# Group 1's operands written where they are multiplied, one transfer for a row's two operands, group 0's second operands in later windows

## The chip, the cores and the metric

The kernel runs on one core of a Trainium2 chip. That core has five engines which each work through a list of instructions of their own in order: PE (products and transposes), DVE and ACT (element-wise work), POOL (here mostly casts) and SP (which issues nearly all transfers). The metric is the device time of one execution in microseconds. The order of every list is fixed when the program is built; what an instruction waits for is a semaphore of another engine or of a transfer.

## The reference

One layer of a hybrid backbone over 2048 latent tokens and 256 context tokens, width 1024:

```python
h  = rmsnorm(x, norm_w)  * (1 + scale) + shift        # 2048 x 1024
hc = rmsnorm(ctx, norm_w) * (1 + scale_c) + shift_c   # 256 x 1024
p, pc = h @ w_in, hc @ w_in[:, :HG_COLS]              # w_in: 1024 x 9216
# 8 heads of 128: S_t = diag(f_t) S_{t-1} + k_t v_t^T, o_t = S_t^T q_t,
# forward and backward, each from the state that the context leaves
y_hg = hgrn_out(o, gate)
y_cv = conv_branch(p[..., HG_COLS:])
y = concatenate([y_hg, y_cv]) @ w_out
return rmsnorm(x + gate_ada * y, final_norm_w)
```

scale, shift and gate come from a small product of the conditioning vector with w_ada ("ada").

## The kernel before

**Tiling.** The 2048 tokens are four groups of 512 (x0 to x3), the context a fifth block of 256. A window is one column block (a head, later a convolution channel block) with one group: head 0 meets groups 0, 1, 2, 3 in windows 0 to 3, and the next blocks run through the groups in turn. A window consists of units, each the product of one pair of 128-column weight blocks with the group. Weights and tokens are held as two float16 halves, hi and lo, and each product is three matmuls: hi by hi, hi by lo, lo by hi (L890 to L892).

**Products.** Most units ("head", "conv") use a scheme of seven products in place of eight on blocks of 2 by 2 (`seven`). A group's side of it are the seven operands B11, T1, T2, B21, T3, B22 and T4, each 512 by 256: the four quarters of h, transposed, and their sums and differences. The names in the trace drop the digits: hop1B is any of window 1's B11, B21 and B22, hop1T any of its T1 to T4. In window 0 the four units are "plain" (eight products, L1419 to L1421), on operands that stay in four tiles hop0. Three "ctx" units (L1405 to L1407) are multiplied with the context's operands, tile hc.

**Making operands.** `norm_group` loads the tokens (L234), squares them on ACT with a sum per row (L238), takes the reciprocal root in a chain of small rows on DVE (L125 to L131), scales the rows on ACT (L244) and DVE (L246), turns them on PE (xT_x, L253), scales by column on ACT (L274), and `combine` makes sums and differences on DVE (L328 to L337). `store2` casts hi on ACT or POOL (L279, L281), subtracts for lo on DVE (L298) and stores the operand to DRAM, tile Hd (L300). One turn is one k of four, that is 128 rows of each half. `prefetch` loads an operand from Hd into one of nine tiles named hop (L1306) when a tile comes free and the group is ready. The second operands of group 0 (T1 to T4), not needed by plain units, are made from a copy of h in DRAM (Xd) by `late_turn`; their tiles on DVE are ha_x, hb_x and ht_x.

**Order.** `run` walks a window's units. Steps of other work, each with a weight (PACE), are placed between its products in proportion to their weight: a chain (the scan of the window before, and head 0's context) and extra steps. Before:

- window 0: four plain and three ctx units; as extra steps the context's norm and turns, x1's norm and turns, x2's loads, norm and first turn;
- window 1: the other turns of x2, then x3's loads, norm and first turn;
- window 2: the other turns of x3;
- window 3: group 0's `late_turn`, four times, and the sums of the final gate (w_ada's last third, gate_r).

A weight pair is loaded, its power-of-two scale taken (ss_p on PE from rb_p on DVE) and split into hi and lo while an earlier unit runs. Head 0's outputs are o_0, o_1 and so on, one for each group, on PE.

The windows' extra steps are chosen here:

```python
early = (ctx_norm[1] + ctx_norm[2] + n1[1] + n1[2] if wi == 0 else n1[2][1:]) + ready_
...
elif wi == NG - 1:
    extra = first[3] + extra
```

Of the kernel before, what the change touches and what calls it, by code (L numbers as in the profile page):

```python
# [9 lines left out]
F32 = mybir.dt.float32  # L10
# [9 lines left out]
P = 128  # L20
# [40 lines left out]
def hybrid_layer(ctx: ExitStack, tc, x, cx, w_ada, b_ada, w_in, w_out, fnorm_w, small_d, masks, ident_d, sel_d, out):  # L61
# [19 lines left out]
    Hd = [{o: dp.tile([P, 2, HK, HW], F16, name=f"Hd{g}{o}", tag=f"Hd{g}{o}") for o in OPS} for g in range(NG)]  # L81
# [32 lines left out]

    def hop_tile(nm):
        return hp.tile([P, 2, HK, HW], F16, tag="hop", name=nm)
# [90 lines left out]
    def modulate_end(pada):  # L207
        ada_r = ring("ada_r")
        V.tensor_copy(ada_r, pada)
        ptr = pa_t("ada_t")  # L210
        for q in range(4):
            PE.transpose(ptr[:, q * P:(q + 1) * P], ada_r[:, q * P:(q + 1) * P], ident)
        V.tensor_tensor(ada, ptr.rearrange("p (q j m) -> p j q m", q=4, j=4)[:, :, :, 0:2],
                        sub(bada, 0, [[4, 4], [1, 4], [0, 2]]), ALU.add)

# [10 lines left out]
    def norm_group(ntile, src, row0, m, nm, first_ops=None, space=q_tile):  # L226
        n = ntile * P
        xs = []
        ssq = sp.tile([P, 16], F32, tag="ssq", name=f"ssq_{nm}", bufs=4)

# [6 lines left out]
        def square(i):  # L237
            S.activation(junk, xs[i], AF.Square, accum_out=ssq[:, i:i + 1])  # L238

        def norm():  # L240
            rstd = rsqrt(ssq[:, :ntile], ntile, 1.0 / D, nm)
# [8 lines left out]
        def transposed(k):  # L250
            pt = pa_t(f"xT_{nm}{k}")
# [4 lines left out]
        def raw(k):  # L256
            pt = transposed(k)
            raws[k] = ring(f"h32_{nm}{k}")
            if k % 2:
# [17 lines left out]
        def cast(eng, hi, src):  # L277
            if eng is G:
                G.tensor_scalar(hi, src, 1.0, 0.0, ALU.mult, ALU.add)  # L279
            else:  # L280
                S.activation(hi, src, AF.Copy)  # L281

        def store(op, k, src, eng):
# [3 lines left out]
            else:  # L287
                hi, lo = [first_ops[k // 2][:, i, k % 2] for i in range(2)]
            cast(eng, hi, src)
            V.tensor_tensor(lo, src, hi, ALU.subtract)  # L290

        def store2(ops, k, row, eng):

            n2 = len(ops)
            pair = hp.tile([P, 2, n2, HW], F16, tag="pair", name=f"hp{ops[0]}_{nm}{k}", bufs=4)
            hi, lo = [pair[:, i].rearrange("p a b -> p (a b)") for i in range(2)]
            cast(eng, hi, row)
            V.tensor_tensor(lo, row, hi, ALU.subtract)  # L298
            for i, op in enumerate(ops):
                SY.dma_start(Hd[row0 // GW][op][:, :, k], pair[:, :, i])  # L300
# [23 lines left out]
        def combine(k, a, b, whole):  # L324
# [10 lines left out]
            else:  # L335
# [8 lines left out]
                [paced(0.0, lambda k=k: raw(k)) for k in range(KT)])  # L344
# [12 lines left out]
    def behind(fn):  # L357

        if not last_keep:
            return fn()  # L360
        with tc.issue_after(last_keep[-1].ins):
            fn()
# [583 lines left out]
    def load_C(pool, tp, names):  # L946

        for o in names:
            C[tp][o] = pool.tile([P, 2, HK, GW], F16, name=f"C{tp}{o}")
# [74 lines left out]
    def wo_at(name, hl, k):  # L1024
        return wo_home(name, hl)[:, k // HK, k % HK, :]
# [160 lines left out]
    for wi, (kind, a, i) in enumerate(stretch):  # L1186
        units, chain, extra = [], [], []
        if kind == "head":
# [4 lines left out]
            if wi == 0:  # L1193
                units += [(zk, "plain", 1, lambda ps, w, s_=sg_: s_.gate_in(0, ps, w)),
                          (zk, "plain", 2, lambda ps, w, s_=sg_: s_.gate_in(1, ps, w)),
                          (vk, "plain", 1, sg_.value_in), (vk, "plain", 2, sg_.query_in),
                          (zk, "ctx", 1, lambda ps, w, c_=c_: c_.gate_in(0, ps, w)),
                          (zk, "ctx", 2, lambda ps, w, c_=c_: c_.gate_in(1, ps, w)), (vk, "ctx", 1, c_.value_in)]
            else:
                units.append((zk, "head", g, sg_.gates))  # L1200
                if i == 0:
                    units += [(zk, "ctx", 1, lambda ps, w, c_=c_: c_.gate_in(0, ps, w)),
                              (zk, "ctx", 2, lambda ps, w, c_=c_: c_.gate_in(1, ps, w))]
                units.append((vk, "head", g, sg_.values))
# [4 lines left out]
            if i == 1:  # L1209
# [8 lines left out]
        if wi > 0 and stretch[wi - 1][0] == "head":  # L1218
            _, pa_h, pi = stretch[wi - 1]
            chain += scan_steps(heads[pa_h], heads[pa_h].segs[pi])  # L1220
# [77 lines left out]
    for wi, g in enumerate(group_of):  # L1298
        if g is not None and wi and g != group_of[wi - 1]:
# [10 lines left out]
    x1_norm = norm_group(NCH, x, GW, 0, "x1", None, wa_hop)  # L1310
    plain = [hp.tile([P, 2, 2, GW], F16, tag="hop", name=f"hop0_{i}") for i in range(KT // 2)]
    a21_ = hop_tile("a21")
    extra_a21 = [[a21_[:, hl, :, i * P:(i + 1) * P] for hl in range(2)] for i in range(2)]
    taken[0] = len(plain) + 1 + NCH
# [11 lines left out]
    pada = modulate(lambda k: first[4][k][1](), lambda: next_w(0))  # L1326
# [272 lines left out]
```

## Time and profile before

| | us |
|---|---|
| median of three runs (lowest, highest) | 2181.78 (2180.26, 2185.07) |
| the profiled run: time, span | 2187.49, 2185.7 |
| PE, PEld busy in the span | 2089.4, 1468.2 |
| DVE, ACT, POOL busy | 1652.1, 1169.2, 157.9 |
| transfers: all 16 engines, mean | 142 GB/s |

The profile is of one execution, which took 2187.49 us. Busy time of an engine leaves out the time in which it waits. A wait is put down to what released it last ("PE xT_x L253 <- DVE xt_x L246": PE's row of line 253 waited for DVE's row of line 246). A row in the timelines has the start, the duration, the engine, the line, what is written and read, and in brackets the idle time just ahead of it. Matmuls overlap: what is shown as 0.27 long starts 0.11 after the one before.

### The profile page before, as it was taken

What the parts mean: (1) busy time and instruction counts of PE and PEld (TensorE: products, weight loads), DVE (VectorE), ACT (ScalarE), POOL (GpSimd) and SP (SyncE); (2) the same over time, 40 slices, a digit from 0 to 9 for tenths busy, and PEclk for the clock granted to TensorE, in tenths of its full rate; (3) what the DMA queues carried; (4) which work ended last, traced back from release to release, by engine and by line L of the source; (5) the groups of instructions that cost most, each with busy time, mean ns of one, the idle gap of its engine ahead of it and who ended that gap; (6) DMA issues with size and microseconds to landing.
All of it is one profiled execution on the core that took longest, in us unless ns stands there. A gap on an engine that the chain in (4) does not pass through costs nothing.

```text
span 2185.7 us, 51899 instructions
## 1 busy us (share of the span) xinstructions
PE 2089.4 (96%) x21563; PEld 1468.2 (67%) x21563; DVE 1652.1 (76%) x3456; ACT 1169.2 (53%) x2341; POOL 157.9 (7%) x239
## 2 busy tenths in 40 slices
PE   5789999999999999999999999999999999999998
PEld 2677688888887988888889887444444444444443
DVE  7887777878779778788687786677787656687775
ACT  7865556666557565666675654344444423333332
POOL 0211111010010110101111000000000000000000
PEclk9999999999999999999999999999999999999999
DMA  9766533433243333333633448923443205633321
GB/s 349 238 205 208 181 132 103 141 116 105 86 159 107 114 114 125 111 108 128 194 123 123 140 156 260 274 97 121 135 139 98 66 30 181 213 124 108 127 85 58
DMA packets 196464, 310.41 MB, mean 142 GB/s; under 512 B 13570, under 2 KB 126594, under 8 KB 194436
## 3 DMA queue, kind: packets, MB, share of 16 engines
q1 hardware_dynamic: 194068, 303.16, 42.5%
q8 instruction: 169, 2.77, 0.5%
q10 hardware_dynamic: 2160, 3.93, 0.5%
q14 instruction: 67, 0.55, 0.1%
HBM read 241.77 MB, written 65.27 MB: 140 GB/s over the span
## 4 chain that ended last, share of the span: by engine, by line
PE 66%; DVE 18%; ACT 8%; DMA 5%; issue 2%; POOL 1%; SPq 0%; POOLq 0%; ACTq 0%; DVEq 0%
PE sa L890 8%; PE sa L891 8%; PE sa L892 8%; PE sb L890 4%; PE sb L891 4%; PE sb L892 4%; PE sa_o L890 2%; PE sa_o L891 2%; PE sa_o L892 2%; DVE e_p L152 2%; PE A L599 2%; PE sc L890 2%; PE sc L892 2%; PE sc L891 2%; DVE K L453 2%
## 5 line engine op out<-in xcount | busy, mean ns | idle before, releaser
L453 DVE TENSOR_TENSOR K<-K,tot 128x512 f32<-128x512 f32 x192 | 133.6, 696 | 60.1 <-PE A L627 27.6
L891 PEld LDWEIGHTS <-e_p 128*128 128x128 f16 x1368 | 134.1, 98 | 60.4 <-issue 10.9
L890 PEld LDWEIGHTS <-e_p 128*128 128x128 f16 x1368 | 134.1, 98 | 59.9 <-DMA hop1T<-Hd1T 2.6
L892 PEld LDWEIGHTS <-e_p 128*128 128x128 f16 x1368 | 134.2, 98 | 52.8 <-issue 1.8
L460 DVE TENSOR_TENSOR Q<-Q,tot 128x512 f32<-128x512 f32 x192 | 132.4, 690 | 44.3 <-PE A L599 30.9
L569 ACT ACTIVATE km<-K 128x512 f32<-128x512 f32 x160 | 109.0, 686 | 69.5 <-DVE K L453 60.0
L890 PEld LDWEIGHTS <-whib_p 128*128 128x128 f16 x912 | 89.3, 98 | 41.2 <-issue 5.0
L890 PEld LDWEIGHTS <-whia_p 128*128 128x128 f16 x912 | 89.4, 98 | 38.5 <-DMA hop3B<-Hd3B 2.8
L891 PEld LDWEIGHTS <-whib_p 128*128 128x128 f16 x912 | 89.4, 98 | 38.2 <-issue 4.1
L891 PEld LDWEIGHTS <-whia_p 128*128 128x128 f16 x912 | 89.3, 98 | 37.7 <-issue 5.6
L892 PEld LDWEIGHTS <-wlob_p 128*128 128x128 f16 x912 | 89.4, 98 | 34.7 <-issue 0.5
L892 PEld LDWEIGHTS <-wloa_p 128*128 128x128 f16 x912 | 89.4, 98 | 34.4
L151 ACT ACTIVATE e_p<-ws_p,sc_p 128x512 f16<-128x512 f32 x108 | 77.2, 717 | 53.4 <-DVE ws_p L413 33.3
L576 POOL COPY qm<-Q 128x512 f32<-128x512 f32 x64 | 55.7, 870 | 630.2 <-DVE Q L460 627.2
L635 POOL COPY A<-Ac 32x128 f32<-32x128 f32 x128 | 68.3, 534 | 371.2 <-ACT A L631 367.2
L897 ACT ACTIVATE u<-sa,sx_w 128x256 f32<-128x256 f32 (+1 forms) x114 | 59.8, 525 | 59.2 <-PE sa L892 48.7
L897 ACT ACTIVATE p<-sb,sx_w 128x256 f32<-128x256 f32 (+1 forms) x114 | 59.4, 521 | 52.9 <-PE sb L892 52.3
L897 ACT ACTIVATE p<-sa,sx_w 128x256 f32<-128x256 f32 (+1 forms) x114 | 59.1, 518 | 47.4 <-PE sa L892 46.6
L152 DVE SCALAR_TENSOR_TENSOR e_p<-ws_p,sc_p,e_p 128x512 f16<-128x512 f32 x108 | 78.5, 742 | 1.0 <-ACT e_p L151 1.0
L813 ACT ACTIVATE cv<-c,small 128x512 f32<-128x512 f32 (+1 forms) x36 | 24.2, 674 | 97.6 <-DVE c L831 52.9
L378 ACT ACTIVATE junk<-ws_p 128x1024 f16<-128x1024 f32 x72 | 75.7, 1051 | 0.2
L151 ACT ACTIVATE hiS_o<-y_o,sc_y 128x1024 f16<-128x1024 f32 x32 | 36.8, 1149 | 72.6 <-PE sa_o L891 32.2
(865 smaller groups left out, 6972.1 us busy)
## 6 DMA issues: line engine op xcount, KB each, us to landing
ws_p<-in_w_in SPq DMA_DIRECT2D x72, 512.0 KB, 4.4
y_o<-yT SPq DMA_DIRECT2D x32, 512.0 KB, 4.2
xt_x<-in_x SPq DMA_DIRECT2D x16, 512.0 KB, 4.6
wa<-in_w_ada SPq DMA_DIRECT2D x16, 512.0 KB, 10.2
Gd<-zs SPq DMA_DIRECT2D x32, 256.0 KB, 3.2
wos<-in_w_out SPq DMA_DIRECT2D x32, 256.0 KB, 3.9
sg<-Gd SPq DMA_DIRECT2D x32, 256.0 KB, 3.8
yT<-y SPq DMA_DIRECT2D x32, 256.0 KB, 2.2
```

What stands on the lines that cost most here:

```text
L151: S.activation(hi, src, AF.Copy, scale=st[:, 0:1])
L152: V.scalar_tensor_tensor(lo, src, st[:, 0:1], hi, ALU.mult, ALU.subtract)
L378: S.activation(junk.rearrange("p (k n) -> p k n", k=KT), stage[i], AF.Abs, accum_out=r)
L453: V.tensor_tensor(m, m, sub(cur, nb + 1, [[2, np_], [-(nb + 1), 2], [0, B]]), ALU.mult)
L460: V.tensor_tensor(m, m, sub(cur, 1, [[2, np_], [nb - 1, 2], [0, B]]), ALU.mult)
L569: S.activation(sub(s.km, 0, [[2 * B, n // (2 * B)], [B, 2], [1, B]]), mix(s.K, n, B, n // (2 * B)), AF.Copy)
L576: G.tensor_copy(sub(qm, 0, [[2 * B, n // (2 * B)], [B, 2], [1, B]]), mix(s.qf, n, B, n // (2 * B)))
L635: G.tensor_copy(A3[js, :, js], s.Ac[js])
L890: PE.matmul(ps, hi[:, k], rh, start=start and k == 0, stop=False, skip_group_check=not start)
L891: PE.matmul(ps, hi[:, k], right(name, 1, k), start=False, stop=False, skip_group_check=not start)
L892: PE.matmul(ps, lo[:, k], rh, start=False, stop=k == nk - 1, skip_group_check=not start)
L897: last_keep.append(S.activation(r, ps, AF.Copy, scale=sx))
```

## The change

1. Group 1's seven operands are written straight into the tiles from which they are multiplied in window 1, own1: four of the hop tiles and three tiles of the kind Q. `store2` has a branch for that (direct): a cast and a difference for each operand of 128x256, and no store. When window 1 begins, `store_own` writes all seven to DRAM, for the later windows. The rows of x1 are loaded into tiles of their own ("stage"), ahead of the context's; x2's go to the tiles that x1 had.
2. The context's squares, norm, turns and its three units move from window 0 to window 1: two units behind the first unit on group 1, the third ahead of the second one. `context_steps` stand in window 1's chain, ahead of the last two scan steps.
3. x2's loads, norm and all four turns stand in window 1, x3's loads and norm at its end or behind, and x3's turns, all four, in window 2.
4. Operands that are made from one row, (B11, T3), (T1, T2) and (B21, B22), share a DRAM tile, Hr, with the halves hi and lo next to each other: one transfer of 128x1024 for a pair instead of two of 256x1x256. A load of an operand that shares a tile is 128x8x256 instead of 128x2048.
5. `late_turn` moves from window 3 to windows 4 and 5, two of the four k in each.
6. At the start: ada_r is copied in halves by DVE and ACT; group 0's last two transposes stand behind ada's, and ACT copies them; the context's half of `affine` stands behind the third of group 0's differences; a group's squares stand behind the casts of the group before and its norm behind that group's differences (`follow`).

The diff, cut:

```diff
+    ROWS = (("B11", "T3"), ("T1", "T2"), ("B21", "B22"), ("T4",))
+    Hr = [{r: dp.tile([P, HK, 2, len(r), HW], F16, ...) for r in ROWS} for g in range(NG)]
+    Hd = [{o: Hr[g][r][:, :, :, i] for r in ROWS for i, o in enumerate(r)} for g in range(NG)]
...
     def modulate_end(pada):
         ada_r = ring("ada_r")
-        V.tensor_copy(ada_r, pada)
+        V.tensor_copy(ada_r[:, :HW], pada[:, :HW])
+        S.activation(ada_r[:, HW:], pada[:, HW:], AF.Copy)
...
         def square(i):
-            S.activation(junk, xs[i], AF.Square, accum_out=ssq[:, i:i + 1])
+            follow(casts.get(before), lambda: S.activation(junk, xs[i], AF.Square, accum_out=ssq[:, i:i + 1]))
 
         def norm():
+            follow(lows.get(before), scaled)
...
         def store2(ops, k, row, eng):
 
             n2 = len(ops)
+            if direct:
+                for i, op in enumerate(ops):
+                    cast(eng, direct[op][:, k, 0], row[:, i * HW:(i + 1) * HW])
+                    low.append(V.tensor_tensor(direct[op][:, k, 1], row[:, i * HW:(i + 1) * HW], direct[op][:, k, 0],
+                                               ALU.subtract))
+                return
...
-            for i, op in enumerate(ops):
-                SY.dma_start(Hd[row0 // GW][op][:, :, k], pair[:, :, i])
+            g = row0 // GW
+            if n2 == 2:
+                SY.dma_start(Hr[g][ops][:, k], pair)
+            else:
+                SY.dma_start(Hd[g][ops[0]][:, k], pair[:, :, 0])
...
-            if i == 1:
+            if i == 1 and wi > 1:
                 chain += context_steps(h)
...
+            scan = scan_steps(heads[pa_h], heads[pa_h].segs[pi])
+            chain += scan[:-2] + context_steps(h) + scan[-2:] if wi == 1 else scan
...
+    for n_, o in enumerate(OPS):
+        own1[o] = hop_tile(f"hop1{o}") if n_ < 4 else qp.tile([P, HK, 2, HW], F16, tag="Q", name=f"hop1{o}", bufs=6)
+    hop[1] = own1
+
+    def store_own():
+        for o in OPS:
+            SY.dma_start(Hd[1][o], own1[o])
...
-            early = (ctx_norm[1] + ctx_norm[2] + n1[1] + n1[2] if wi == 0 else n1[2][1:]) + ready_
+            early = [paced(25.0, lambda: None)] + n1[1] + n1[2] + ready_ if wi == 0 else n1[2] + ready_
...
+            if wi == 1:
+                store_own()
+                for _, st in n1[0]:
                     st()
-                early += [paced(0.1, store_first)]
-            if n2 is not None:
-                early += [paced("pause", lambda: None)]
-                if wi == 0:
-                    early += [paced(0.1, lambda: next_w(1, 6))]
-                else:
-                    early += n2[0]
-                early += n2[1] + n2[2][:1]
+                taken[0] += NCH
+                early = [paced(w_ / 3, fn_) for w_, fn_ in ctx_norm[1] + ctx_norm[2] + n1[1]] + early
+            if n2 is not None and wi:
+                early += [paced("pause", lambda: None)] + n2[0] + n2[1]
             extra = early + extra
-        elif wi == NG - 1:
-            extra = first[3] + extra
+        elif wi in (NG, NG + 1):
+            extra = first[3][(wi - NG) * 2:(wi - NG) * 2 + 2] + extra
```

What stands in a row shows in the lists of the engines. First PE before, between the last context unit of window 0 (tile u, read from hc) and window 1's first product (tile sa, read from hop1B; xt_x are x2's scaled tokens, xT_x their transposes):

```order
L1407 LDWEIGHTS wloa_p_277
L1407 MATMUL u_1123<-hc,wloa_p_277 128x256
L253 MATMUL xT_x_1082<-ident,xt_x_488 128x128
L253 MATMUL xT_x_1089<-ident,xt_x_488 128x128
L253 MATMUL xT_x_1082<-ident,xt_x_490 128x128
L253 MATMUL xT_x_1082<-ident,xt_x_492 128x128
L253 MATMUL xT_x_1089<-ident,xt_x_490 128x128
L253 MATMUL xT_x_1089<-ident,xt_x_492 128x128
L253 MATMUL xT_x_1181<-ident,xt_x_488 128x128
L253 MATMUL xT_x_1082<-ident,xt_x_494 128x128
L253 MATMUL xT_x_1089<-ident,xt_x_494 128x128
L253 MATMUL xT_x_1181<-ident,xt_x_490 128x128
```
```order
L890 LDWEIGHTS whia_p_219
L890 MATMUL sa_1164<-hop1B_1013,whia_p_219 128x256
```

And PE now, at the first product of window 1 (u is the last plain unit's, read from group 0's tile hop):

```order
L1458 MATMUL u_775<-hop_3_141,whib_p_266 128x256
L1459 LDWEIGHTS wlob_p_267
L1459 MATMUL u_775<-hop_3_141,wlob_p_267 128x256
L917 LDWEIGHTS whia_p_207
L917 MATMUL sa_888<-hop1B_474,whia_p_207 128x256
```

Window 1's first product stands behind the last plain one, with no context unit and none of x2's transposes in front. Next the transfers on SP before, where group 1's operands go to DRAM and come back (hpB_x and hpT_x are the pairs just made):

```order
L300 DMA Hd1T_98<-hpB_x_968 256x1x256
L300 DMA Hd1B_97<-hpB_x_973 256x1x256
L300 DMA Hd1B_99<-hpB_x_973 256x1x256
L1306 DMA hop1B_1013<-Hd1B_94 128x2048
L300 DMA Hd1T_100<-hpT_x_979 256x1x256
L1306 DMA hop1T_1015<-Hd1T_95 128x2048
```

And SP now, at the start of window 1:

```order
L1374 DMA Hd1B_91<-hop1B_474 1024x1x256
L1374 DMA Hd1T_92<-hop1T_475 1024x1x256
L1374 DMA Hd1T_92<-hop1T_476 1024x1x256
L1374 DMA Hd1B_93<-hop1B_477 1024x1x256
L1374 DMA Hd1B_91<-hop1T_478 1024x1x256
L1374 DMA Hd1B_93<-hop1B_479 1024x1x256
L1374 DMA Hd1T_94<-hop1T_480 128x2048
L252 DMA xt_x_878<-in_x 128x1024
```

The loads of hop1 are gone; seven stores stand in front of the loads of x2's tokens. Last, DVE before in window 3, around the row rb_p for the scale of a weight pair:

```order
L337 TENSOR_TENSOR hb_x_2758<-hb_x_2758,ht_x_2761 128x256
L607 COPY_PREDICATED Ac_2_2751<-mask,A_0_2_2980 128x128 x2
L298 TENSOR_TENSOR hpT_x_2764<-ht_x_2761,hpT_x_2764 128x512
L298 TENSOR_TENSOR hpT_x_2770<-ha_x_2757,hpT_x_2770 128x256
L298 TENSOR_TENSOR hpT_x_2775<-hb_x_2758,hpT_x_2775 128x256
L328 TENSOR_TENSOR ht_x_2824<-ha_x_2820 128x256
L382 TENSOR_TENSOR rb_p_3025<-rsum_p_2978,rsum_p_3023 128x1
```

And DVE now, at the same place:

```order
L480 TENSOR_TENSOR K_2_1870<-K_2_1870,tot_2_2614 128x16x2x16
L487 TENSOR_TENSOR Q_2_2426<-Q_2_2426,tot_2_2614 128x16x2x16
L634 COPY_PREDICATED Ac_2_2672<-mask,A_0_2_2848 128x128 x2
L409 TENSOR_TENSOR rb_p_2893<-rsum_p_2846,rsum_p_2891 128x1
L431 TENSOR_TENSOR ws_p_863<-ws_p_861,ws_p_863 128x512
```

The row rb_p follows the scan's own rows; group 0's second operands (ha_x, hb_x, ht_x) don't stand there any more.

More of the change, by code (lines that the diff above doesn't have):

```diff
@@ L224, in affine, with follow, norm_group @@
         V.tensor_scalar(ab[:, m], ab[:, m], hsc[m][:, 0:1], None, ALU.mult)
-    def norm_group(ntile, src, row0, m, nm, first_ops=None, space=q_tile):
+    def follow(marks, fn):
+        if not marks:
+            return fn()
+        with tc.issue_after(marks[-1].ins):
+            fn()
+    lows, casts = {}, {}
+    def norm_group(ntile, src, row0, m, nm, first_ops=None, space=q_tile, direct=None):
         n = ntile * P
@@ L229, in norm_group @@
         ssq = sp.tile([P, 16], F32, tag="ssq", name=f"ssq_{nm}", bufs=4)
+        before = None if first_ops is not None else "x1" if m else f"x{row0 // GW - 1}"
+        low, high = lows.setdefault(nm, []), casts.setdefault(nm, [])
         def load(i):
@@ L357, in behind @@
     def behind(fn):
[L359 to L362, printed above, removed]
+        follow(last_keep, fn)
     def load_pair(col0, col1, nm, own=False, a21_at=None):
@@ L1324, in hybrid_layer @@
     next_w(0)
[L1326 removed]
+    pada = modulate(lambda k: first[4][k]() if k < KT - 2 else None, lambda: next_w(0))
     ctx_norm = norm_group(2, cx, 0, 1, "c")
[L1328 removed]
+    for _, st in x1_norm[0] + ctx_norm[0]:
         st()
[L1330 removed]
+    turned = modulate_end(pada)
+    for k in (KT - 2, KT - 1):
+        follow(turned, first[4][k])
     affine(0, 7)
@@ L1445, in run @@
             pace[1] += 1
-        if wi == 0 and units[-1][1] == "ctx" and len(units) > 2:
+        if wi == 0:
             freed[0] += 5
```

79 lines of the change are left out of this document (41 added, 38 removed).

## The prediction

> **What bounds the kernel now.** I read the page's first part, then its chain of work that ended last, then the table by windows over the first 328 us, then PE's waits there, and last the timelines of PE, ACT and DVE at the longest of them. The page and its chain:
>
> ```profile
> PE 2089.4 (96%) x21563; PEld 1468.2 (67%) x21563; DVE 1652.1 (76%) x3456; ACT 1169.2 (53%) x2341; POOL 157.9 (7%) x239
> PE 66%; DVE 18%; ACT 8%; DMA 5%; issue 2%; POOL 1%; SPq 0%; POOLq 0%; ACTq 0%; DVEq 0%
> ```
>
> PE is busy 2089.4 of 2185.7 us, and the change takes no product away, so it can win only from the other 96.3 us and from time in which PE runs at a lower granted clock. By windows (start:end and length, then busy us of PE, PEld, DVE, ACT and POOL, granted clock, DMA share, GB/s):
>
> ```profile
> 55.00:82.00 27.00, 26.45 (x236) 23.17 (x235) 21.59 (x54) 24.71 (x44) 6.60 (x12) 1.00 0.75 236
> 82.00:110.00 28.00, 15.65 (x175) 13.39 (x175) 24.86 (x60) 22.11 (x38) 6.49 (x8) 0.81 0.76 242
> 110.00:137.00 27.00, 23.40 (x317) 18.94 (x316) 25.02 (x60) 18.00 (x36) 5.50 (x7) 0.88 0.69 222
> 219.00:273.00 54.00, 49.24 (x597) 36.00 (x598) 42.67 (x93) 31.59 (x59) 6.21 (x8) 1.00 0.59 180
> 273.00:328.00 55.00, 53.73 (x746) 46.81 (x744) 42.87 (x108) 32.31 (x95) 6.19 (x11) 1.00 0.40 133
> ```
>
> The loss lies where the change works: 12.35 us of PE idle in 82 to 110 and 3.6 in 110 to 137, at a clock of 0.81 and 0.88, while DVE is busy 24.86 of 28 and 25.02 of 27 us. From 273 us on PE loses 1.27 in 55. PE's waits from 40 to 260 us (us in total, times, longest):
>
> ```profile
> PE xT_x L253 <- DVE xt_x L246: 8.0, 2, 7.1
> PE u L1419 <- ACT hop L281: 2.6, 1, 2.6
> PE u L1405 <- ACT f_c L496: 2.5, 1, 2.5
> PE sa L890 <- DMA hop3B<-Hd3B: 2.5, 1, 2.5
> PE ss_p L139 <- DVE rb_p L382: 2.5, 1, 2.5
> PE sa L890 <- DMA hop1T<-Hd1T: 2.5, 1, 2.5
> ...
> PE sc L890 <- ACT q L543: 0.9, 1, 0.9
> ...
> PE sa L890 <- ACT p L897: 0.6, 1, 0.6
> ...
> PE sa L890 <- DMA hop1B<-Hd1B: 0.3, 1, 0.3
> ```
>
> The round trip of group 1 through DRAM is waited for only twice, 0.3 and 2.5 us. The longest wait is for group 2's scaled rows, whose transposes stand ahead of window 1's first product.
>
> **Term 1, the start: -2.5.** ACT's timeline ahead of the first product, then DVE's:
>
> ```profile
> 42.27 1.06 ACT L238 ACTIVATE junk<-xt_c 128x1024 f16<-128x1024 f32 x1 [2.15 <-DMA xt_c<-in_ctx]
> 43.23 0.19 ACT L238 ACTIVATION_READ_ACCUMULATOR junk<-xt_c 128x1 f32 x1
> 43.32 0.80 ACT L270 ACTIVATE h_x<-h_x,ab 128x512 f32<-128x512 f32 x1
> ...
> 38.74 0.69 DVE L260 COPY h_x<-xT_x 128x512 f32<-128x512 f32 x1 [0.75 <-PE xT_x L253]
> 39.35 0.68 DVE L209 COPY ada_r<-pada 128x512 f32<-128x512 f32 x1
> 40.84 0.19 DVE L213 TENSOR_TENSOR ada<-ada_t,small 128x32 f32<-128x32 f32 x1 [0.81 <-PE ada_t L212]
> ```
>
> ACT sits in the context's square, which waited 2.15 us for its load, until 43.32; only then does it scale group 0's rows, and PE's first plain product waits 2.6 us for the cast behind that. The context's squares leave, which frees ACT at about 42.3 or before. The row L209 no longer stands behind the last two transposes' copies (1.3 us from 38.74), and it is halved between two engines (0.3 of its 0.68 us). That is about 1.6 us on the chain of ada, and the second half of the affine chain, which interleaves its rows with the first from 41.1 to 42.7, leaves with some 0.8 us. Sum 2.4 to 2.7; I take 2.5. The two copies moved behind go to ACT ahead of the last operands, where they can take back 1.4 (two like L260's 0.69); hence 1 to 3.5.
>
> **Term 2, windows 0 to 2: -2.5.** PE's timeline around the two worst places:
>
> ```profile
> 94.35 2.42 PE L253 MATMUL xT_x<-ident,xt_x 128*128 128x128 f32 x10 [7.07 <-DVE xt_x L246]
> 97.06 0.37 PE L890 MATMUL sa<-hop1B,whia_p 128*128 128x256 f16 x1 [0.30 <-DMA hop1B<-Hd1B]
> ...
> 99.71 0.27 PE L892 MATMUL sa<-hop1B,wloa_p 128*128 128x256 f16 x1
> ...
> 109.71 0.27 PE L890 MATMUL sa<-hop1T,e_p 128*128 128x256 f16 x1
> 109.82 0.37 PE L891 MATMUL sa<-hop1T,e_p 128*128 128x256 f16 x1
> ...
> 119.92 0.36 PE L891 MATMUL sa<-hop1B,whia_p 128*128 128x256 f16 x1
> ```
>
> What goes: the waits for xt_x (8.0), f_c (2.5), hop1B (0.3) and hop1T (2.5), 13.3 us. Behind them products run at half pace (0.42 shown for 0.27, starts 0.21 apart for 0.11) from 94.35 to 99.7 and from 109.82 to 119.92: 5.3 us, half of it lost, and 10.1 us, of which some 2.6 are waits and half of the rest is lost: 2.6 + 3.7 = 6.3. Together **19.6**.
>
> The price of making operands is read from DVE's groups, 193 to 250 us, where it makes group 0's second ones (count | us, mean ns | idle before):
>
> ```profile
> L298 DVE TENSOR_TENSOR hpT_x<-ht_x,hpT_x 128x512 f16<-128x512 f32 x4 | 2.9, 737 | 0.0
> ...
> L298 DVE TENSOR_TENSOR hpT_x<-ha_x,hpT_x 128x256 f16<-128x256 f32 x4 | 2.1, 517 | 0.0
> L329 DVE TENSOR_TENSOR ht_x<-hb_x,ht_x 128x256 f32<-128x256 f32 x4 | 1.7, 422 | 0.1
> L328 DVE TENSOR_TENSOR ht_x<-ha_x 128x256 f32<-128x256 f32 x4 | 1.7, 419 | 1.3 <-DMA ha_x<-Xd 1.3
> ...
> L337 DVE TENSOR_TENSOR hb_x<-hb_x,ht_x 128x256 f32<-128x256 f32 x4 | 1.7, 418 | 0.0
> L331 DVE TENSOR_TENSOR ha_x<-hb_x,ha_x 128x256 f32<-128x256 f32 x4 | 1.7, 418 | 0.0
> L298 DVE TENSOR_TENSOR hpT_x<-hb_x,hpT_x 128x256 f16<-128x256 f32 x4 | 1.7, 414 | 0.5 <-POOL hpT_x L279 0.5
> ```
>
> What comes in place, walked through the new order with the durations of the trace:
> - Group 1's last row of operands. All casts and differences now end ahead of the multiplication itself, seven pieces of 128x256 instead of three of 512 and one of 256. From the rows of L298, 0.74 for 512 and 0.42 to 0.52 for 256, that is about 3 us a row instead of 2.7. Window 1's first product stands straight behind the plain ones, at some 73 us, and DVE ends group 1 at 77 to 81. The product starts on the first three k while the fourth is made: 1.5, between 0 and 4.
> - Weight unit 2's sum (ss_p) now stands behind the fourth product, and its row rb_p behind group 1's on DVE. Nearest row: the same wait in window 3, 2.5. I take 2.5 (0 to 4).
> - The context's units need 12 differences (hc) that DVE mixes with a weight pair's split. Nearest row: f_c's 2.5, and 12 by 0.42 is 5.1. I take 3.5 (0 to 7).
> - Group 2's transposes stand behind two of these units and one product, and still wait for loads that are issued behind seven stores, for squares, and for the norm: 4, between the 0.9 that is the second of the two waits in 8.0 and the 7.1 that is the first.
> - Group 2's operands are now all made in window 1, so its round trip is met in window 2 as hop1T's was: 2 (0 to 5). Group 3's last rows wait for tiles that group 1's operands hold: 1 (0 to 3).
> - Half pace behind the longest of these: one spell like the first, 2.6 (0 to 6.3).
>
> Sum 1.5 + 2.5 + 3.5 + 4 + 2 + 1 + 2.6 = **17.1**, net -2.5. A check by place: the context's third unit and group 2's first transposes leave the stretch before head 0's first output, and group 2's and 3's come behind it, so the two outputs that follow come earlier by unequal amounts (some 10 us and 5 us with term 1), not by the same.
>
> How PE runs slow is the point where a rule bears on the sum. The row at 109.71 is at full pace and the next at 109.82 is not, 1.1 us behind a wait of only 2.5 us. The Trainium skill, TensorE: Matmul & The Clock Gate, Part 1 (the clock gate), says that the default is throttled, that about 3.4 us of sustained work releases it, and that idle gaps longer than about 3.4 us are what to avoid. By that page waits of 1.5 to 3.5 us would cost no clock, the 2.6 would be 0, and the sum would be 2.6 us better. The trace disagrees: a 2.5 us wait is followed by a slow spell, and the spells last 5.3 and 10.1 us. I keep the rows.
>
> **Term 3, window 3: -3.9.** Group 0's second operands leave it. Their rows, shown in term 2, sum to 13.5 us of DVE. The row rb_p, for which PE waits 2.5 us, stands behind fifteen of them in the order of before. I count as gone that wait and two short ones of the same window, for q (0.9) and for p (0.6, cut to 0.5 as it is ACT's): 3.9. The wait for hop3B (2.5) is a transfer's and stays, the loads of w_ada too. Ends: 0 (another engine is as late) and 6.4 (hop3B's goes too).
>
> **Term 4, windows 4 and 5: +2.** Half of the 13.5 us goes to each. DVE there has 42.87 of 55 us; with 6.75 it has 49.6, 90%, as in 82 to 137 where PE waits, but here nothing of the start is in its way and PE stands idle 1.27. If each window gets back a part of the 2.5 for rb_p, 1 us each: +2 (0 to 5).
>
> **At nothing**: stores and loads. A pair of rows goes in one transfer instead of two, and SP has 766 rows for 822. Loads of operands are now read in pieces of 512 B instead of 4 KB. For both shapes there are rows (KB each, median us to landing):
>
> ```profile
> q1 hardware_dynamic: 194068, 303.16, 42.5%
> ...
> hop2T<-Hd2T SPq DMA_DIRECT2D x4, 512.0 KB, 5.1
> ...
> C0T<-Hd0T SPq DMA_DIRECT2D x4, 512.0 KB, 5.9
> C0T<-Hd1T SPq DMA_DIRECT2D x4, 512.0 KB, 7.2
> ```
>
> C0T is read in 256-element pieces as the new operands are, and lands 0.8 to 2.1 us later than hop2T. From window 6 on a product of 12 matmuls at 0.11 lasts 1.3 us and a tile comes free nine products ahead, 11.8 us: that hides it. Without that cover it would be 0.8 to 2.1 for each load that is late, 7 in a window. The queue's row gives 42.5% of 16 x 2185.7 us over 194068 packets, 77 ns for a mean of 1562 B. The Trainium skill, DMA: Bandwidth & Descriptors, Specifications, puts the least transfer for full rate at 512 B; by that page the pieces cost nothing even in window 2, and its term would be 1 lower. The C0T rows speak against it, though they also differ in what runs beside them.
>
> **Sum**: -2.5 - 2.5 - 3.9 + 2.0 = -6.9 on the profiled run's own 2187.49 us (span 2185.7 and 1.8 around it), 2180.6. That run is 0.26% above the median of the three, 2181.78; carried there, **2174.9**.
>
> **The rivals.**
> - *The waits only change places.* Group 2 inherits group 1's hand-off: its rows wait 7.1 instead of 4, its transfer 2.5 instead of 2, the context's differences 5.1 instead of 3.5. Term 2 is then 19.6 - 22.3 = +2.7, the sum -1.7, and the time about 2180. For it: DVE has the same rows up to head 0's second output and is 90% busy there. Against: the x1 path loses its transfer, and PE has work ahead of each wait. Chance 0.29.
> - *The path of before was longer than its waits.* If DVE's rows for group 2 and the context fall into PE's own work, the new waits halve (17.1 to 8.6) and the sum is -15: about 2167. For it: before, the 7.1 us wait had window 1's first products behind it, which didn't need what was waited for. Against: DVE's 90%. The rule on the clock lies on this side too. Chance 0.17.
> - *Slower: group 3 comes late.* Its rows are loaded into tiles that hold group 1's T3, B22 and T4, so the loads are issued behind group 2's on SP, its first turn has left window 1, and all four turns stand in window 2. If the last load lands 8 us later than the turns want it, hop3B's wait of 2.5 grows by those 8, with a slow spell of 2.6 behind it: -6.9 + 10.6 = +3.7, and with term 4 at its upper end +6.7, about 2188.5. It decides from a delay of about 9 us (past 4.4 slower). Chance 0.13.
> - The forecast, 0.41.
>
> **How the numbers follow.** 0.2% of the time, 4.4 us, is about what a measurement of this kernel tells from no change. Faster holds the forecast and the second rival, 0.58; the first rival lies within, 0.29; the third is slower, 0.13. The range runs from below the second rival, with 3 us for the error of its terms, 2164, to 2187, short of the third: about 2 in 10 lie outside.
>
> **What would show it.** The first product of group 3 before, on PE:
>
> ```profile
> 197.09 0.28 PE L890 MATMUL sa<-hop3B,whia_p 128*128 128x256 f16 x1 [2.49 <-DMA hop3B<-Hd3B]
> ```
>
> Term 1: the first plain product 2.5 earlier than before. Term 2: no wait for hop1 at all; one for xt_x of about 4, near 105; head 0's first output some 10 us earlier, and the row above about 5 us earlier. Term 3: no wait for rb_p in window 3, but still one for hop3B. Term 4: PE idle 2 to 4 us in windows 4 and 5. I am wrong if the first product of group 3 starts at 197.09 or later, or if windows 4 and 5 lose more than window 3 wins.

## The result, and the profile after

The changed kernel is **slower**: 2203.54 us median (2199.91 to 2204.82, six runs) against 2186.18 us for the kernel before in the same rounds, a ratio of 1.0081 with a 95% interval of 1.0069 to 1.0093, some 17.7 us. The profiled run's span is 2201.5 us, 15.8 more than before.

The page after, its first part and its chain, has nearly the same shares:

```profile
PE 2097.9 (95%) x21563; PEld 1473.0 (67%) x21563; DVE 1653.3 (75%) x3467; ACT 1172.7 (53%) x2351; POOL 161.1 (7%) x243
PE 66%; DVE 18%; ACT 7%; DMA 4%; issue 3%; POOL 1%; SPq 1%; POOLq 0%; ACTq 0%; DVEq 0%
```

A loss of 0.8% doesn't show in shares. The table by windows has its place (columns as before):

```profile
55.00:82.00 27.00, 22.87 (x193) 19.68 (x192) 20.79 (x53) 22.15 (x42) 7.17 (x12) 0.93 0.34 114
82.00:110.00 28.00, 19.13 (x260) 14.52 (x257) 25.28 (x73) 23.17 (x44) 6.57 (x10) 0.95 0.64 211
110.00:137.00 27.00, 20.87 (x249) 17.61 (x250) 22.23 (x53) 16.51 (x30) 5.96 (x10) 0.86 0.32 110
137.00:164.00 27.00, 24.85 (x203) 20.81 (x202) 14.56 (x34) 13.24 (x27) 1.64 (x2) 0.95 0.78 223
164.00:219.00 55.00, 41.88 (x527) 34.89 (x525) 39.76 (x88) 29.59 (x52) 8.36 (x14) 0.88 0.50 153
...
273.00:328.00 55.00, 53.20 (x762) 45.66 (x761) 48.44 (x115) 32.61 (x83) 8.88 (x15) 1.00 0.66 199
```

And two of the rows of before that the prediction doesn't show:

```profile
137.00:164.00 27.00, 23.69 (x256) 20.14 (x253) 21.40 (x52) 16.32 (x28) 4.56 (x8) 0.94 0.53 184
164.00:219.00 55.00, 50.76 (x796) 43.60 (x794) 40.92 (x88) 31.46 (x60) 9.90 (x14) 1.00 0.64 209
```

In 82 to 110 PE is busy 3.5 us more, as the change meant, but 3.6 less in 55 to 82 and 2.5 less in 110 to 137. In 164 to 219 it is busy only 41.88 of 55 us, before 50.76, and in the stretch just ahead, 137 to 164, DVE is busy only 14.56 of 27, before 21.40. PE's waits from 40 to 260 us:

```profile
PE xT_x L274 <- DVE xt_x L267: 4.9, 2, 3.1
PE sa L917 <- DVE vT L928: 3.8, 1, 3.8
PE sa L918 <- DVE hop1B L319: 2.6, 1, 2.6
PE sb L917 <- DVE f L928: 2.6, 1, 2.6
...
PE A L626 <- DVE Q L487: 2.1, 2, 1.3
PE sb L917 <- ACT p L924: 1.9, 1, 1.9
PE A L654 <- DVE Q L487: 1.8, 1, 1.8
PE u L1444 <- DVE hc L311: 1.6, 1, 1.6
```

No wait is as long as the 7.1 of before; there are many short ones, some 24 of 39 us in all for DVE.

Where the time goes is best read from the start of the first product on each group's operands, in each kernel's view of the tiles (us; hop2 is group 2 in window 2, hop3 group 3 in windows 3 and 4, hop5 and hop6 belong to windows 5 and 6, hop34 to 34, C0T to the stage behind all of them):

| kernel | hop2 | hop3 | hop5 | hop6 | hop34 | C0T | span |
|---|---|---|---|---|---|---|---|
| before | 155.8 | 197.1 | 286.9 | 319.8 | 1320.1 | 1371.2 | 2185.7 |
| after | 153.8 | 215.0 | 297.1 | 331.8 | 1332.2 | 1390.7 | 2201.5 |
| difference | -2.0 | +17.9 | +10.2 | +12.0 | +12.1 | +19.5 | +15.8 |

So: 19.9 us are lost in window 2, 7.7 come back in windows 3 and 4, 1.8 go in window 5, nothing happens for a thousand microseconds, and 7.4 are lost around window 35. The 3.7 that return behind C0T don't look like a gain of the change: from C0T to the end the changed kernel takes 810.8 us and the ten kernels of the experiments take 809.7 to 812.9, while before's profiled run takes 814.5, with a wait of 2.4 us for p and slow products behind it.

**Window 2.** SP's timeline of the changed kernel (start, how long SP was at it, what):

```profile
145.75 0.34 SPq L252 DMA_DIRECT2D xt_x<-in_x  x1
147.83 0.32 SPq L330 DMA_DIRECT2D Hd2T<-hpT_x  x1
148.25 0.58 SPq L1334 DMA_DIRECT2D hop2B<-Hd2B  x1
148.92 2.09 SPq L1334 DMA_DIRECT2D hop2T<-Hd2T  x2
151.06 1.58 SPq L1334 DMA_DIRECT2D hop2B<-Hd2B  x1
152.69 1.74 SPq L1334 DMA_DIRECT2D hop2T<-Hd2B  x1
154.47 3.09 SPq L1334 DMA_DIRECT2D hop2B<-Hd2B  x1
157.65 1.70 SPq L1334 DMA_DIRECT2D hop2T<-Hd2T  x1
159.40 0.93 SPq L252 DMA_DIRECT2D xt_x<-in_x  x2
```

Before, the last operand of group 2 was stored at 133.98 and its loads went out one by one until 143.10:

```profile
133.98 0.57 SPq L300 DMA_DIRECT2D Hd2T<-hpT_x  x1
134.64 0.56 SPq L1306 DMA_DIRECT2D hop2B<-Hd2B  x1
...
143.10 0.32 SPq L1306 DMA_DIRECT2D hop2T<-Hd2T  x1
```

Now the last store is at 147.83, the seven loads stand in one burst behind it, and from the fourth on each holds SP for 1.6 us and more. Group 3's last two token loads are behind them, at 159.4. ACT's and DVE's rows show who waits:

```profile
167.04 1.06 ACT L256 ACTIVATE junk<-xt_x 128x1024 f16<-128x1024 f32 x1 [3.01 <-DMA xt_x<-in_x]
...
170.14 0.17 DVE L131 TENSOR_SCALAR rsv_x<-ssq_x 128x4 f32<-128x4 f32 x1 [4.85 <-ACT junk L256]
```

ACT squares the late tokens at 167, DVE starts group 3's norm at 170.14. Before, that norm began at 135.39:

```profile
135.39 0.16 DVE L125 TENSOR_SCALAR rsv_x<-ssq_x 128x4 f32<-128x4 f32 x1
```

In stretches of ten microseconds, first before, then after:

```profile
150.00:160.00 10.00, 9.22 (x108) 8.47 (x106) 7.88 (x18) 4.97 (x11) 2.48 (x4) 0.96 0.40 120
160.00:170.00 10.00, 9.25 (x141) 8.09 (x140) 8.29 (x17) 6.56 (x13) 1.87 (x3) 1.00 0.40 119
...
180.00:190.00 10.00, 10.00 (x103) 9.18 (x101) 7.69 (x12) 5.74 (x11) 4.13 (x6) 1.00 0.46 145
190.00:200.00 10.00, 7.51 (x69) 6.67 (x68) 6.82 (x19) 3.59 (x7) 0.45 (x1) 1.00 0.85 283
```
```profile
150.00:160.00 10.00, 9.19 (x82) 8.12 (x81) 3.67 (x9) 5.58 (x11) 0.00 (x0) 1.00 1.13 284
160.00:170.00 10.00, 8.92 (x80) 7.46 (x79) 1.45 (x3) 3.38 (x7) 0.00 (x0) 1.00 0.75 243
...
180.00:190.00 10.00, 4.90 (x96) 3.80 (x96) 9.56 (x20) 6.48 (x11) 2.47 (x4) 1.00 0.45 151
190.00:200.00 10.00, 6.74 (x99) 5.31 (x100) 9.54 (x20) 3.09 (x5) 2.59 (x6) 0.54 0.45 134
```

DVE (the third count of busy us and rows) does 5.1 us of work in 150 to 170 instead of 16.2, and then has all of group 3's turns and the scan at once: 9.56 and 9.54 of 10, while PE falls to 4.90 and 6.74, in the second at a granted clock of 0.54. This is DVE work moved into the wrong place, not more of it (1653.3 us against 1652.1 in all).

**Window 35.** There the loads for hop35 stand on SP behind eight loads of the next stage, in both kernels. Now the last four loads of hop34 ahead of them hold SP for 1.6 to 2.5 us each, before for 0.3 to 0.7. PE's timeline after:

```profile
1358.20 0.39 PE L917 MATMUL sb<-hop35T,whib_p 128*128 128x256 f16 x1 [3.63 <-DMA hop35T<-Hd3T]
...
1367.86 0.27 PE L917 MATMUL sb<-hop35B,e_p 128*128 128x256 f16 x1 [2.08 <-DMA hop35B<-Hd3B]
```

PE's waits for hop35 before, from 1300 to 1420 us:

```profile
PE sa L890 <- DMA hop35T<-Hd3T: 0.7, 1, 0.7
...
PE sc L890 <- DMA hop35B<-Hd3B: 0.2, 1, 0.2
```

### The profile page after: what moved, and what is told of

The parts are those of the page before. It is cut to its first block, busy times and chain, and to the rows that moved or that the text cites. A ratio compares the mean times of both kernels' runs of the same rounds, so it can differ in the third digit from the quotient of the medians.

```text
span 2201.5 us, 51795 instructions
## 1 busy us (share of the span) xinstructions
PE 2097.9 (95%) x21563; PEld 1473.0 (67%) x21563; DVE 1653.3 (75%) x3467; ACT 1172.7 (53%) x2351; POOL 161.1 (7%) x243
## 4 chain that ended last, share of the span: by engine, by line
PE 66%; DVE 18%; ACT 7%; DMA 4%; issue 3%; POOL 1%; SPq 1%; POOLq 0%; ACTq 0%; DVEq 0%
PE sa L917 8%; PE sa L919 8%; PE sa L918 8%; PE sb L917 4%; PE sb L918 4%; PE sb L919 4%; PE sa_o L917 2%; PE sa_o L918 2%; PE sa_o L919 2%; PE sc L917 2%; DVE e_p L158 2%; PE A L626 2%; PE sc L918 2%; PE sc L919 2%; DVE Q L487 2%
## 5 line engine op out<-in xcount | busy, mean ns | idle before, releaser
L918 PEld LDWEIGHTS <-whia_p 128*128 128x128 f16 x912 | 89.8, 98 | 40.8 <-issue 7.9
```

The costliest lines, as they stand in the source:

```text
L918: PE.matmul(ps, hi[:, k], right(name, 1, k), start=False, stop=False, skip_group_check=not start)
```

## The experiments

Two suspects: the form of the loads (pieces), and the order in which group 3's tokens come. Each ratio is to the kernel before in the same rounds, so ratios compare across experiments; the changed kernel's is 1.0081. In the diffs n1 and n2 are the next two groups' steps: [0] the loads, [1] the norm, [2] the four turns.

**Operands apart again.** One store and one load for each operand, as in the kernel before; hi and lo stay next to each other as in the changed one:

```diff
-    Hr = [{r: dp.tile([P, HK, 2, len(r), HW], ...) for r in ROWS} for g in range(NG)]
-    Hd = [{o: Hr[g][r][:, :, :, i] for r in ROWS for i, o in enumerate(r)} for g in range(NG)]
+    Hd = [{o: dp.tile([P, HK, 2, HW], ...) for o in OPS} for g in range(NG)]
...
-                SY.dma_start(Hr[g][ops][:, k], pair)
+            for i, op in enumerate(ops):
+                SY.dma_start(Hd[g][op][:, k], pair[:, :, i])
```

> The changed kernel with every operand in a DRAM tile of its own again: two stores for a row's two operands, and loads that read 4 KB in one piece instead of eight of 512 B; all else is kept. Theory P (pieces): the loads of 512-byte pieces take SP 1.6 us each to issue when seven stand in a row (11 us from 148.3 to 159.4), so group 3's last two token loads behind them are late, and the same happens to window 35's loads. Then here the seven take some 4 us, group 3's first product comes 7 to 9 us earlier than 215.0, window 35 loses its extra 6.7, and the time falls by 13 to 16, to about 2188 to 2190. Theory O (order): group 3 is late because its loads stand behind group 2's and all its four turns stand in window 2, whatever the pieces are. Then group 3's first product stays within 3 us of 215.0, only window 35 gains, and the time falls by 6 to 8, to about 2196.

Measured: 2192.5 us, ratio 1.0035 (1.0022 to 1.0048), some 10 us below the changed kernel. hop3 starts at 209.6, 5.4 earlier; from hop34 to C0T it is 52.3 us, against 58.5 after and 51.1 before. SP's timeline of this run:

```profile
148.12 0.38 SPq L1331 DMA_DIRECT2D hop2B<-Hd2B  x1
148.56 1.16 SPq L1331 DMA_DIRECT2D hop2T<-Hd2T  x2
...
150.25 0.57 SPq L1331 DMA_DIRECT2D hop2T<-Hd2T  x1
150.86 0.44 SPq L1331 DMA_DIRECT2D hop2B<-Hd2B  x1
151.79 0.32 SPq L1331 DMA_DIRECT2D hop2T<-Hd2T  x1
152.16 1.22 SPq L251 DMA_DIRECT2D xt_x<-in_x  x2
```

The seven loads take SP 4.0 us instead of 11.1, and the tokens are issued 7.2 us earlier. But they are in use only 3.4 us earlier; the transfer engines are full until then. The table by windows of this run and ACT's row for the tokens:

```profile
150.00:160.00 10.00, 9.16 (x84) 8.30 (x83) 3.35 (x8) 5.80 (x11) 0.00 (x0) 1.00 1.03 410
...
163.60 1.06 ACT L255 ACTIVATE junk<-xt_x 128x1024 f16<-128x1024 f32 x1 [0.37 <-DMA xt_x<-in_x]
```

The result lies between the theories: pieces cost about 10 us, more than O allowed and less than P wanted. That the tokens still stand behind 3.5 MB of operands, whatever the form, fits the rows (issued at 152.16, in use at 163.60).

**Order on SP.** Tokens ahead of group 2's last operands, pieces kept:

```diff
+            if held[0] and queue[0][0] == 2 and OPS.index(queue[0][2]) >= 3:
+                break
...
-                early += [paced("pause", lambda: None)] + n2[0] + n2[1]
+                early += [paced("pause", lambda: None)] + n2[0] + ([paced(0.0, release)] if wi == 1 else []) + n2[1]
```

> The changed kernel with group 3's last two token loads put on SP behind the third and fourth of group 2's operand loads instead of behind the seventh; pieces of 512 B are kept. Theory O: the last token load is issued at about 155 instead of 159.9, norm and turns follow 5 us earlier, group 3's first product starts at about 209 to 210, and the time falls by 5 to 6. Theory P: the tokens come as much earlier, but group 2's last operands are later by as much, so the gain is 2 to 4; window 35 keeps its loss. A third theory, D: group 3 is bound by DVE and by the products of its window, not by its tokens; then the time stays within 2 us.

Measured: 2197.95 us, 1.0058 (1.0042 to 1.0075), 5 us below the changed kernel; hop3 at 208.1, and window 35 kept its loss (57.6 us from hop34 to C0T). The 5 us have an error of some 4.5 by the two intervals, so the time doesn't tell O (5 to 6) from P (2 to 4). hop3, 6.9 earlier, is on O's side, and D fell: group 3 was late at least in part because its tokens were.

**Group 0's second operands back in window 3**, with the line of the kernel before:

```diff
-        elif wi in (NG, NG + 1):
-            extra = first[3][(wi - NG) * 2:(wi - NG) * 2 + 2] + extra
+        elif wi == NG - 1:
+            extra = first[3] + extra
```

> The changed kernel with group 0's second operands back in window 3, all four. All theories: window 3, from group 3's first product to its last, is longer by 5 to 8 us (it was 73.8 before and 66.1 after), windows 4 and 5 shorter by 1 to 2; the time rises by 4 to 6, to about 2208. If the 7.7 us that window 3 won came from something else, for example from tokens that are late for it in any case, the time stays within 2 us.

Measured: 2207.35 us, 1.0105 (1.0082 to 1.0128), about 5 above. From hop3 to hop5 (windows 3 and 4) 91.1 us against 82.1; from hop5 to hop6 (window 5) 32.9 against 34.7. That move was a gain, as the part alone, further down, shows more sharply.

**Pairs alone on the kernel before**; here hi and lo stay apart, as in that kernel:

```diff
-            for i, op in enumerate(ops):
-                SY.dma_start(Hd[row0 // GW][op][:, :, k], pair[:, :, i])
+            if n2 == 2:
+                SY.dma_start(Hr[g][ops][:, :, k], pair)
+            else:
+                SY.dma_start(Hd[g][ops[0]][:, :, k], pair[:, :, 0])
```

> The kernel before with one part of the change alone: the two operands of a row share a DRAM tile, one store for a pair, and loads in pieces of 512 B. Theory P: window 35's loads lose 5 to 7 us as in the changed kernel, and the loads of groups 1, 2 and 3 that are waited for in windows 1 to 3 lose 1 to 3 each: 6 to 12 us slower than before, about 2192 to 2198. Theory O: pieces cost nothing that counts; within 2 us of before.

Measured: 2192.97 us, 1.0039 (1.0026 to 1.0052), 8.5 us slower than before. hop3 starts at 197.8, hop5 at 290.7 (3.1 us lost in windows 3 and 4), and hop34 to C0T takes 56.0 (4.9 lost). PE's waits from 1300 to 1420 us in this run:

```profile
PE sb L896 <- DMA hop35T<-Hd3T: 3.7, 1, 3.7
...
PE sb L896 <- DMA hop35B<-Hd3B: 1.4, 1, 1.4
```

The layout of the pairs alone costs half of what the whole change costs, within theory P's range. But not where P looked first: window 2 takes 41.5 us, as before (41.3). Group 2's loads have pieces of 512 B here too, but they go out as tiles come free, and most of them hold SP no longer than 0.52 us:

```profile
134.79 0.57 SPq L1312 DMA_DIRECT2D hop2B<-Hd2B  x1
...
141.92 0.52 SPq L1312 DMA_DIRECT2D hop2T<-Hd2B  x1
```

**Tokens early.** What is left once the tokens are really early? They need tiles of the kind Q, and in the changed kernel three of these hold T3, B22 and T4, which window 1 finishes last. Swapped:

```diff
-        own1[o] = hop_tile(f"hop1{o}") if n_ < 4 else qp.tile(...)
+        own1[o] = hop_tile(f"hop1{o}") if n_ > 2 else qp.tile(...)
...
-                    if o and final and (wi > 1 or OPS.index(o) < 4):
+                    if o and final and (wi > 1 or OPS.index(o) > 2):
```

> The changed kernel with the homes of group 1's operands swapped: B11, T1 and T2, which window 1's last unit finishes first, lie in the three tiles of the kind Q, the other four in hop tiles. Group 3's token loads, which need Q tiles, then all stand ahead of group 2's operand loads on SP; pieces of 512 B are kept. Theory H (late tokens leave DVE idle from 150 to 170 and crowd it from 180 to 210): tokens landed by about 152, the norm on DVE at about 155 instead of 170, DVE busy over 6 of 10 us in 160 to 170, group 3's first product at 203 to 206 instead of 215.0, and the time falls by 9 to 12, to about 2192. Theory D2 (window 2 is bound by the four turns and the scan on DVE whenever the tokens come): group 3's first product at 208 or later, as when the loads stood behind four of the seven, and the time falls by 5 to 6.

Measured: 2192.15 us, 1.0031 (1.0021 to 1.0042), 11 us below the changed kernel. hop3 starts at 201.3, 13.7 earlier. DVE's row for the norm, and DVE in the table by windows:

```profile
152.08 0.17 DVE L131 TENSOR_SCALAR rsv_x<-ssq_x 128x4 f32<-128x4 f32 x1 [0.61 <-ACT junk L256]
...
160.00:170.00 10.00, 8.25 (x131) 6.95 (x129) 9.37 (x19) 6.35 (x13) 3.33 (x5) 1.00 0.71 234
```

The norm is 18 us earlier, DVE is busy 9.37 us of 10 in 160 to 170 instead of 1.45. Theory H held (hop3 came even earlier than its 203 to 206); D2 fell. With pieces of 512 B kept, hop34 to C0T still takes 57.0.

**Both**, swapped homes and operands apart, and group 3's loads written ahead of `set_ready`, the step that lets group 2's operands be loaded:

```diff
-            early = ... if wi == 0 else n1[2] + ready_
+            early = ... if wi == 0 else n1[2] + (n2[0] if n2 else []) + ready_
...
-                early += [paced("pause", lambda: None)] + n2[0] + n2[1]
+                early += [paced("pause", lambda: None)] + n2[1]
```

> The changed kernel with both: operands in DRAM tiles of their own (loads in one piece of 4 KB) and the swapped homes, with group 3's token loads ahead of group 2's operands. Theories P and H together: group 3's first product at 199 to 203, window 35 without its loss, time 15 to 18 below the changed kernel, 2186 to 2189, within 0.3% of before. If pieces and late tokens are the whole of the loss, and the shorter window 3 stays (7.7, less 1.8 in windows 4 and 5), it is 2180 or below: faster than before.

Measured: 2185.58 us, 0.9998 (0.9988 to 1.0007): all 18 us are gone, and no more than those. hop3 starts at 203.4, still 6.3 later than before. From hop2 to hop3 it takes 48.8 us, as with swapped homes alone (48.7), and from hop34 to C0T 50.1 instead of 57.0: with early tokens the pieces cost nothing in window 2, and 6.9 us around window 35.

**And group 3's first turn back in window 1**:

```diff
-            early = ... else n1[2] + (n2[0] if n2 else []) + ready_
+            early = ... else n1[2][wi - 1:] + (n2[0] if n2 else []) + ready_
...
-                early += [paced("pause", lambda: None)] + n2[1]
+                early += [paced("pause", lambda: None)] + n2[1] + n2[2][:1]
```

> As the run before, and group 3's first turn back in window 1, behind its norm, as in the kernel before. Theory H: what is left of the delay is DVE's work of that turn (4.2 us by the rows of a turn) in window 2; group 3's first product 3 to 5 us earlier than in the run before, time 2182 to 2185. Theory D3: the turn in window 1 holds up head 0's first output by as much, since tokens land at about 152 at the earliest; no gain, or a loss of 2 to 4.

Measured: 2183.54 us, 0.9993 (0.9984 to 1.0003). hop3 comes 2.3 earlier, at 201.1, but hop2 4.2 later, at 158.8: between H and D3, and no difference that can be measured, neither from before nor from the run without the turn.

**Parts alone on the kernel before.** Which parts are worth having? Tried were the line for windows 4 and 5, the start's edits (diff as in the change, point 6, without `follow` on squares and norms), and both.

```diff
-        elif wi == NG - 1:
-            extra = first[3] + extra
+        elif wi in (NG, NG + 1):
+            extra = first[3][(wi - NG) * 2:(wi - NG) * 2 + 2] + extra
```

> The kernel before with one part of the change alone: group 0's second operands are made in windows 4 and 5, two rows in each, instead of all four in window 3. If the 7.7 us that window 3 won in the changed kernel are this part's: group 3's first product stays at 197 within 1 us, window 5's first comes 6 to 8 us earlier than 286.9, windows 4 and 5 give back about 2, and the time is 4 to 6 below before (0.2 to 0.3%). If window 3 was shorter only because it began 18 us late, with its weights and loads long there: within 2 us of before.

Measured: 2179.8 us, 0.9979 (0.9970 to 0.9988), 4.6 us faster. Windows 3 and 4 take 86.3 us instead of 89.8, window 5 34.3 instead of 32.9. That is half of the 7.7 that the changed kernel won in windows 3 and 4. hop3 starts 1.8 earlier than in before's profile already, hop2 1.7 and the first plain product 0.4, and nothing is changed ahead of them: two executions can differ by that much there, and less of a difference in one start is not to be read.

> The kernel before with the start's edits alone (ada_r in two halves, group 0's last two transposes behind ada's, the context's half of the affine chain behind the third difference). The first plain product 0.8 to 2 us earlier than 44.69 (2.3 in the changed kernel, where the context's squares have left too). If PE carries that on: time 1 to 2 below before. If the waits of windows 0 and 1 (group 2's norm, 7.1) take it back: no change.

Measured: 2182.66 us, 0.9990 (0.9982 to 0.9999), some 2 us. The first plain product starts at 43.42, 1.3 earlier. No change lies just outside the interval.

> Both parts on the kernel before. If they add: 5 to 8 below before (about 0.3%), faster than both kernels. If the start's part is taken back, the same as the run with late operands alone.

Measured: 2176.42 us, 0.9969 (0.9957 to 0.9980), 6.8 us faster than before and 24 faster than the changed kernel: the fastest of all. The parts add, as far as the intervals can tell (4.6 and some 2 us alone).

The landmarks of all runs:

| kernel | hop2 | hop3 | hop5 | hop6 | hop34 | C0T | ratio |
|---|---|---|---|---|---|---|---|
| operands apart | 155.0 | 209.6 | 294.9 | 329.0 | 1329.0 | 1381.3 | 1.0035 |
| order on SP | 154.5 | 208.1 | 292.5 | 327.0 | 1330.7 | 1388.3 | 1.0058 |
| second operands back | 154.3 | 212.3 | 303.4 | 336.3 | 1336.8 | 1394.1 | 1.0105 |
| pairs alone | 156.3 | 197.8 | 290.7 | 323.6 | 1324.5 | 1380.5 | 1.0039 |
| homes swapped | 152.6 | 201.3 | 284.4 | 319.8 | 1322.0 | 1379.0 | 1.0031 |
| apart and swapped | 154.6 | 203.4 | 288.6 | 322.6 | 1323.1 | 1373.2 | 0.9998 |
| and first turn back | 158.8 | 201.1 | 286.4 | 320.4 | 1320.1 | 1372.1 | 0.9993 |
| late operands alone | 154.1 | 195.3 | 281.6 | 315.9 | 1316.2 | 1368.8 | 0.9979 |
| start alone | 152.5 | 193.0 | 284.5 | 317.4 | 1318.1 | 1370.2 | 0.9990 |
| late and start | 153.6 | 194.4 | 279.4 | 313.6 | 1313.2 | 1363.8 | 0.9969 |

## Why the prediction was wrong

**Wrong: the part "at nothing", for loads in pieces of 512 B.** It looked for cover in the steady windows, found 11.8 us there, and cover is what they had: from hop6 to hop34 before and after differ by 0.1 us. It didn't ask where loads stand in a burst or behind another burst. The changed kernel has two such places, window 2 and window 35. Undoing the pieces there is worth 10 us. Adding them to the kernel before costs 8.5, by the landmarks 4.9 around window 35, 3.1 in windows 3 and 4 and 0.2 in window 2, where the loads are no burst. In window 2 they cost by way of the tokens behind them: with the tokens ahead the pieces cost nothing there. The row for it was at hand: C0T's loads, of the same form, landed 0.8 to 2.1 us later than hop2T's, and I took the lower of two readings, that this hides.

**Wrong: term 2's last two items, group 2's round trip at 2 (0 to 5) and group 3's tokens at 1 (0 to 3).** The step from hop2 to hop3 lost 19.9 us, and hop3 starts at 215.0, past the 197.09 that I had named as the sign of being wrong. I priced each as a wait on PE. The tokens' delay is not one wait: it leaves DVE idle for 15 of 20 us and crowds it afterwards, and PE pays in many waits of 1 to 2 us (13.5 us from 160 to 220, against 4.0 before; 4.6 of them for the scan's rows Q that stand between group 3's turns), at a slow clock in part. With the tokens early 10.9 of the 17.7 us are gone. I had this mechanism as the third rival, with the right cause (loads behind group 2's on SP, all four turns in window 2), at a chance of 0.13 and a price of some 10.6, half of what it took. What I missed is that the change makes the seven loads one burst: before, they were issued from 134 to 143 as tiles came free.

**Wrong: head 0's first output some 10 us earlier.** Its first row (o) came at 151.9 instead of 153.9, and hop2, which follows it, 2.0 earlier too, no more than term 1's gain. Of the waits that I listed most are there, near the size given (group 2's xt_x 3.1 for 4, hop1B 2.6 for 1.5, hc 1.6 for 3.5); those for hop1's loads and for rb_p are not. But there are others, on the products' results (vT 3.8, f 2.6), that I hadn't listed. And this though both engines have less to do ahead of hop2 than before: PE 994 rows instead of 1068, DVE 119.8 us instead of 126.2. With both defects mended (0.9998) the change is where it started, though it holds the two parts that alone are worth 0.31%; so, if the parts add as they did alone, what is left of the change (points 1 to 3, mainly) costs some 0.3% net, here and in this form. The landmarks of that run say where: from hop2 to hop3 it takes 48.8 us instead of 41.3, and DVE is busy 40.2 us of them instead of 32.5, with work that lay ahead of hop2 before; hop2 comes only 1.2 earlier for it. With the first turn put back the step takes 42.3, but hop2 is 4.2 later. Why the time ahead of hop2 doesn't shrink as DVE's work there does was not taken apart.

**Right: term 1**, -2.5: the first plain product starts at 42.35 instead of 44.69, 2.3 earlier; 1.3 of it comes with the edits alone, of which 0.4 lies within what two executions differ by.

**Right: terms 3 and 4**, -3.9 and +2. Alone on the kernel before, windows 3 and 4 win 3.5 (forecast for both 3.9 less 1) and window 5 loses 1.4 (forecast 1). As forecast, the changed kernel has no wait for rb_p in window 3 and one for hop3B (1.5); PE is idle only 1.3 us in its windows 4 and 5, against 2 to 4 forecast. That the 7.7 in the changed kernel is more because its window 3 starts late, with more already done, is not shown.

**The clock.** I kept the rows against the rule to avoid idle gaps over about 3.4 us (the Trainium skill, TensorE: Matmul & The Clock Gate, Part 1), read as if shorter ones cost no clock. The runs bear the rows out: in 190 to 200 of the changed kernel the granted clock is 0.54, and no wait of PE in the 30 us ahead of it is longer than 1.93 us.

## What to carry to other kernels

A layout that saves stores has to be priced on the loads, at the places where loads stand in a burst, not in the steady state. Work that is moved to a later window takes its inputs with it: look at which tile and which place in the issuing queue each input needs, and when these come free. A gap on an engine that isn't the bound can be where the bound engine's later waits come from; here DVE's gap in 150 to 170 was paid by PE in 180 to 200. And a change of many parts should be run part by part: two of these six were worth 0.31%, together with the others the gain was lost.

## What the runs showed of the hardware

Pieces of 512 B fill the transfer engines at a lower rate: in 150 to 160 us the changed kernel's transfer share is 1.13 at 284 GB/s, that with pieces of 4 KB has 1.03 at 410 (a share of about 1 or more: all 16 engines are busy). The Trainium skill (DMA: Bandwidth & Descriptors, Specifications) gives 512 B as the least transfer for full rate; here it isn't enough, by some 30%. And SP feels it: a load of 512 KB in such pieces holds it for 0.52 us alone (0.32 in pieces of 4 KB, hop9's loads after and before), but for 1.6 to 3.1 us as the fourth or later of the burst, against 0.3 to 0.6 in pieces of 4 KB. What stands behind the burst in SP's list, here group 3's tokens, is late by that: issued at 159.4 instead of 152.2.
